# A two-layer encoder on one core: the exchange of the softmax's sums issued by ScalarE, the gate of heads 4 to 7 with its operands kept in SBUF, and another order of x's norms and of the second layer's transpositions

## The chip, the core and the metric

The kernel runs on one core of a Trainium2 chip. A core has a matrix engine (TensorE, PE in the profile), a vector engine (VectorE, DVE), a scalar engine (ScalarE, ACT), a general engine (GpSimd, POOL) and a synchronisation engine that here does little but issue transfers (SyncE, SP). Each engine works through its own instructions in order and stops at the first whose semaphore has not been reached; the instruction that issues a DMA is one of them. The tensors lie in SBUF (128 partitions); TensorE writes its results into banks of PSUM. The metric is the device time of one execution in microseconds, as the median of several runs.

## The reference

For 512 tokens of width 1024 two layers are computed, all in float32. Each normalises x, makes one wide projection, mixes heads, lets four heads attend to 256 memory tokens, gates everything and projects back. The first layer's mixer is the part that the change touches most: eight heads, each with three window attentions of different dilation, whose outputs are joined by a softmax over their log-sum-exps.

```python
o_g, l_g = dilated_window_attention(q[:, :, g], k[:, :, g], v[:, :, g], window, dilation)
...
o = jnp.stack(outs, axis=2)
w = jax.nn.softmax(jnp.stack(lses, axis=2), axis=2)
o = jnp.sum(w[..., None].astype(o.dtype) * o, axis=2)
...
y = jnp.concatenate([o_mix, o_mem], axis=-1) * jax.nn.silu(gate)
x = x + jnp.einsum('bse,ed->bsd', y, w_out[i])
```

The second layer's mixer is a grouped-query attention (8 query heads, 2 key heads) with rotary positions.

## The kernel before, in words

**Products.** A float32 product is made from three fast ones: each operand is split into a rounded part and a remainder ("hi" and "lo"). For a weight piece of 128x1024 (`wl`, loaded from DRAM) ScalarE makes the rounded part (`wh`, line 333, line 331 for the memory's weights) and VectorE the remainder (`wo`, line 347). TensorE then runs lines 178, 179 and 182: `wh` with the activations' two parts, `wo` with their rounded part. The rings of `wh` and `wo` hold four pieces each. Each chunk of 512 columns is computed with seven products in place of eight (the function `s_chunk`), whose summed weights GpSimd makes by accumulating DMAs (lines 260, 296, 306) and whose results ScalarE (line 415) and VectorE (lines 428, 438) take out of PSUM.

**Order.** Every engine's order is fixed when the program is written. The class `Driver` counts slots, about one weight piece each; work beside the projections sits in generators which give back how many slots are to pass until they go on (`yield 3`). In a slot `drv.soon` puts an operation at its beginning, `drv.late` at its end. The first layer goes through heads 0 to 7, then the gate of heads 4 to 7 (`b`), the gate of the memory's heads (`m`) and that of heads 0 to 3 (`a`); a head takes about 49 us.

**The exchange.** The three dilations of a head keep their tokens in two layouts across partitions: natural and strided by four. Each softmax needs the maxima and sums of both, so they are exchanged through a small DRAM buffer `ds`. VectorE packs them into `stp` (line 1494, 128 partitions x 16 numbers); SyncE writes both halves to `ds` (lines 1496 and 1497, 512 pieces of 8 bytes and 128 of 32 bytes), and `Y[3]` slots later reads them back in the other layout into `oth` (lines 1499 and 1500). The reads wait for the writes' landing. VectorE goes on from `oth` at line 1505. SyncE also issues nearly all loads of weights (line 260), the stores of the heads' outputs `od` (line 1353) and the loads of gathered values (lines 1483 to 1485), all in one order.

**The gate.** A head's output `o` goes to DRAM (`od`) and is loaded back when its gate is computed, unless it is in `DIRECT`: then it stays in SBUF. Line 911 multiplies two heads at once from a joint load, line 915 one head.

**Beginnings.** The first layer's activations are normalised in `setup` and `prep` (line 583 by VectorE), transposed, and combined for the seven products in `diffs_t` and `rest_t` (ScalarE lines 650, 655, 671, VectorE 675, 677, 672; tiles `f`, `fS` and their split parts `hS`). In the second layer `ev_rot` norms, rotates and transposes queries and keys (TensorE line 708, four 128x128 transpositions into one bank, then ScalarE line 1724 and VectorE line 1725).

Of the kernel before, what the change touches and what calls it, by code (L numbers as in the profile page):

```python
# [25 lines left out]
MEM_STEP = 1, 1  # L26
MEM_D = 4
PAUSE = 2
DIRECT, DIRECT_B = (6, 7), (3, 4, 5, 6, 7)
LO_K, TURN_K, HI_V, LO_V = (4, 4), (8, 5), (1, 6), (9, 2)  # L30
PD = 2
WARM = 6, 5
# [101 lines left out]
def trunk_kernel(ctx: ExitStack, tc: tile.TileContext, x, mem, wall, norm_g, mem_norm_g, gcol,  # L134
                 qn_a, kn_a, qn_b, kn_b, ident_d, mask_d, tab_a, tab_b, out):
    nc = tc.nc
# [515 lines left out]
    def diffs_t(H, low, c, view=same, turn=same, late=False):  # L652

        f22 = whole("22", c)
        A.copy(view(f22), turn(turn4(low[1], None, None)))
        p = turn(turn4(low[0], None, None))
        yield 1
        s1, s3 = whole("S1", c), whole("S3", c)
        V.tensor_tensor(view(s1), p, view(f22), ALU.subtract)
        V.tensor_tensor(view(s3), view(full["11", c]), p, ALU.subtract)  # L660
        hl = slot(H, "S1", c)
        if late:
            drv.late(lambda: split(*hl, s1))
        else:
            split(*hl, s1)
# [202 lines left out]
    def gates(od, o_done, o_here, direct, fused=False, turn=None):  # L868
# [3 lines left out]
        def gate(H, first, g, half=False):  # L872


            pre = {}
            if g < 2:
                yf[g] = [m4(name="yf") for _ in range(2)]
                if fused:
                    assert all(first + n in o_done for n in range(4))
                    for j in range(2):  # L880
                        pre[j] = m4(name="og").rearrange("p (h t) -> p h t", h=2)
                        nc.scalar.dma_start(pre[j], od[first + 2 * j:first + 2 * j + 2].rearrange("h p t -> p h t"))

            def ev(q, u, t):
                i, j = int(q[0]) - 1, int(q[1]) - 1
                h0, ts = first + 2 * j, slice(i * 256, (i + 1) * 256)
                hs, got, asked = (h0, h0 + 1), {}, []
                tv = t.rearrange("p (h t) -> p h t", h=2)

                def load():  # L890
                    if "o" not in got and all(h in o_done for h in hs):
                        asked.append(h0)
                        o = got["o"] = s2(name="og")
                        nc.sync.dma_start(o.rearrange("p (h t) -> p h t", h=2), od[h0:h0 + 2, :, ts].rearrange("h p t -> p h t"))
                        got[h0] = got[h0 + 1] = o.rearrange("p (h t) -> p h t", h=2)
                    for n, h in enumerate(hs):
                        if h in got:
                            continue
                        if h in o_here:
                            got[h] = o_here[h][:, None, ts].to_broadcast([128, 2, 256])  # L900
                        elif h in o_done and (hs[1 - n] in direct):
                            o = s2(name="og")[:, 0:256]
                            nc.sync.dma_start(o, od[h, :, ts])
                            asked.append(h)
                            got[h] = o[:, None, :].to_broadcast([128, 2, 256])

                def times(dst):
                    if "pre" in got:
                        V.tensor_tensor(dst.rearrange("p (h t) -> p h t", h=2), tv, got["pre"], ALU.mult)
                    elif "o" in got:  # L910
                        V.tensor_tensor(dst, t, got["o"], ALU.mult)
                    else:
                        dv = dst.rearrange("p (h t) -> p h t", h=2)
                        for n, h in enumerate(hs):
                            V.tensor_tensor(dv[:, n], tv[:, n], got[h][:, n], ALU.mult)

                if pre:
                    for h in hs:
                        got[h] = got["pre"] = pre[j][:, :, ts]
                else:  # L920
                    load()
                th = s2(name="th")
                A.activation(th, t, AF.Tanh, scale=0.5)
                yield 1
                V.scalar_tensor_tensor(t, th, 1.0, t, ALU.add, ALU.mult)
                yield 1
                if not all(h in got for h in hs):
                    load()
                    while not all(h in got for h in hs):
                        yield 1  # L930
                        asked.clear()
                        load()
                    if asked if fused else not all(h in o_here for h in hs):
                        yield 1
                if g < 2:
                    times(yf[g][j][:, i * 512:(i + 1) * 512])
                    y_done.add((g, i, j))
                    return
                times(t)
                if not fused:  # L940
                    yield 1
                ys[2 * j + i] = t

            s_chunk(256, H, ev, tokens=False, half=half, soon=g == 2, turn=turn)
# [265 lines left out]
    def prep():  # L1210

        for c in range(5):
            if c > 1:
                norm_2(xb[c - 1], n[c - 1], rows["x"])
            if 1 < c < 4:
                n[c] = norm_1(xb[c], c == 2)
            if 1 < c < 4:
                first_t(H, xb[c - 2], c - 2, by_class, from_rows)
            yield 1

        def forms(c):
            yield from diffs_t(H, xb[2 + c], c, by_class, from_rows)
            yield 3
            yield from rest_t(H, c, (2, 2, 2))

        drv.spawn(forms(1), 1)
        yield from forms(0)
# [32 lines left out]
    def square(b, j, act=True):  # L1260

        if act:
            A.activation(s2(name="sq"), mb[b][j], AF.Square, scale=1.0 / 32.0, accum_out=ss[b][:, j:j + 1])
        else:
            V.tensor_tensor_reduce(s2(name="sq"), mb[b][j], mb[b][j], 1.0 / 1024.0, 0.0, ALU.mult, ALU.add, ss[b][:, j:j + 1])
# [9 lines left out]
    def place_m(b, j, act=True):  # L1275

        p = turn4(mb[b][j], None, None)
        split(*[M.block(n, j, slice(b * 128, (b + 1) * 128)) for n in range(2)], p, act)
# [19 lines left out]
    def ahead(u, b):  # L1298

        if (u, b) == (0, 0):  # L1300
            square(1, 0)
            square(0, 1, False)
            place_m(1, 0)
            W.hi(True)
            W.hi(True)
        if (u, b) == (0, 1):
            place_m(0, 1)
            factor(0)
            square(1, 1, False)
            place_m(1, 1)  # L1310
            factor(1)
            n[0] = norm_1(xb[0])
            n[1] = norm_1(xb[1])
        if (u, b) == (1, 0):
            norm_2(xb[0], n[0], rows["x"])

    drv.spawn(prep(), PD)
    drv.spawn(setup(), SET_AT)
# [111 lines left out]
    def attn_a(h, qk0, qs, ks, v12, n_done):  # L1430
# [62 lines left out]
        oth = small.tile([128, 2, 4, 2], F32, tag="oth", name="oth", bufs=2)  # L1493
        V.tensor_copy(stp, st.rearrange("p o s b -> p o b s"))
        yield 1
        nc.sync.dma_start(nat_v[0], stp[:, 0])
        nc.sync.dma_start(str_v[1], stp[:, 1].rearrange("p b s -> p (b s)"))
        yield Y[3]
        nc.sync.dma_start(oth[:, 0], nat_v[1])
        nc.sync.dma_start(oth[:, 1].rearrange("p b s -> p (b s)"), str_v[0])  # L1500
        yield Y[4]
        own = stp.rearrange("p o b s -> p (o b) s")
        oth_ = oth.rearrange("p o b s -> p (o b) s")
# [210 lines left out]
        V.tensor_tensor(x[:, :, 64:128], ta[:, :, 64:128], sb[:, :, 0:64], ALU.add)  # L1714
        yield d[2]

    def ev_rot(t, qk, tab, hi, lo, d):
        n = t.shape[-1] // 128
        r = head_sq(t, n)
        yield d[0]  # L1720
        head_mul(t, r, n, dst=t)
        yield from rope_b(t, qk, tab, d)
        p = turn_h(t) if tab[1] > 1 else transpose4(t.rearrange("p (a e) -> p a e", e=128), n)[:, 0:n]
        drv.late(lambda: A.copy(hi, p))
        drv.soon(lambda: V.tensor_tensor(lo, p, hi.bitcast(F32), ALU.subtract))
        yield 1

    kbT = [m4(F32R, "kbT").rearrange("p (h t) -> p h t", h=2) for _ in range(2)]
    vb = [m4(F32R, "vb").rearrange("p (b e) -> p b e", b=4) for _ in range(2)]
    qs_b = [[[m4(F32R, "qb").rearrange("p (h t) -> p h t", h=4) for _ in range(2)] for _ in range(2)]]  # L1730
    k_done, q_done = {}, set()

    def ev_qkv(q, u, t):
        i, j = int(q[0]) - 1, int(q[1]) - 1
        b = 2 * i + u
        cs = slice(b * 128, (b + 1) * 128)
        if j:
            hi, lo = [v[:, b] for v in vb]
            A.activation(hi, t[:, 256:512], AF.Copy, scale=0.5)
            yield from ev_rot(t[:, 0:256], 1, (b, 1), *[v[:, :, cs] for v in kbT], YB["k"])  # L1740
            V.scalar_tensor_tensor(lo, t[:, 256:512], 0.5, hi.bitcast(F32), ALU.mult, ALU.subtract)
            k_done[b] = drv.slot
        else:
            cs = slice(u * 128, (u + 1) * 128)
            yield from ev_rot(t, 0, (b, 1), *[v[i][:, :, cs] for v in qs_b[0]], YB[0])
            q_done.update((0, b, j) for j in range(2))
# [204 lines left out]
```

## Time and profile before

| | |
|---|---|
| median of 3 runs | 934.84 us (933.46 to 935.6) |
| the profiled execution | 934.63 us |
| its span | 932.9 us, granted TensorE clock 0.999 |
| VectorE busy | 800.9 us, 86% of the span |
| ScalarE busy | 696.4 us, 75% |
| GpSimd busy | 361.2 us, 39% |
| share of the 16 DMA engines: SyncE's queue (q1), GpSimd's (q0), ScalarE's (q10) | 42.1%, 38.9%, 1.0% |

The span runs from the first to the last instruction of the profile; the profiled execution's own time is 1.7 us longer. Rows of the trace name start, duration, engine, line, operation and tiles (written one first); "ACTq" or "SPq" is an instruction that issues a transfer. In brackets stands the idle time ahead of an instruction and what ended it.

### The profile page before, as it was taken

What the parts mean: (1) busy time and instruction counts of PE and PEld (TensorE: products, weight loads), DVE (VectorE), ACT (ScalarE), POOL (GpSimd) and SP (SyncE); (2) the same over time, 40 slices, a digit from 0 to 9 for tenths busy, and PEclk for the clock granted to TensorE, in tenths of its full rate; (3) what the DMA queues carried; (4) which work ended last, traced back from release to release, by engine and by line L of the source; (5) the groups of instructions that cost most, each with busy time, mean ns of one, the idle gap of its engine ahead of it and who ended that gap; (6) DMA issues with size and microseconds to landing.
All of it is one profiled execution on the core that took longest, in us unless ns stands there. A gap on an engine that the chain in (4) does not pass through costs nothing.

```text
span 932.9 us, 16288 instructions
## 1 busy us (share of the span) xinstructions
PE 925.0 (99%) x5471; PEld 814.6 (87%) x5471; DVE 800.9 (86%) x1452; ACT 696.4 (75%) x1730; POOL 361.2 (39%) x504
## 2 busy tenths in 40 slices
PE   9999999999999999999999999999999999999998
PEld 7789888888888888888889998888988999999886
DVE  6999677878888888979798989999898998789977
ACT  7875789676868686867776667757879887789774
POOL 4311424556564646464746102234262440110122
PEclk9999999999999999999999999999999999999999
DMA  9999957968686878686867999999985686785777
GB/s 347 393 261 332 294 133 202 328 151 241 163 248 158 261 159 271 158 270 130 252 156 190 285 267 262 293 322 335 295 204 113 178 241 169 198 219 127 196 167 181
DMA packets 83723, 213.38 MB, mean 229 GB/s; under 512 B 18992, under 2 KB 26296, under 8 KB 83640
## 3 DMA queue, kind: packets, MB, share of 16 engines
q1 hardware_dynamic: 61288, 141.68, 42.1%
q0 software_dynamic: 20384, 67.12, 38.9%
q10 hardware_dynamic: 1968, 3.54, 1.0%
q8 instruction: 43, 0.70, 0.3%
q14 instruction: 40, 0.33, 0.1%
HBM read 163.23 MB, written 12.91 MB: 189 GB/s over the span
## 4 chain that ended last, share of the span: by engine, by line
PE 91%; DVE 4%; ACT 2%; issue 1%; DMA 1%; POOL 1%; SPq 0%; DVEq 0%; ACTq 0%; POOLq 0%
PE pj L178 24%; PE pj L179 24%; PE pj L182 24%; PE qT L708 3%; PE sa L1462 2%; PE oo L1571 2%; PE ptb L1780 1%; PE sa L1458 1%; DVE wo L347 1%; PE pt L1550 1%; PE ob L182 1%; PE ob L179 1%; PE ob L178 1%; PE sb L173 1%; PE sb L172 1%
## 5 line engine op out<-in xcount | busy, mean ns | idle before, releaser
L347 DVE TENSOR_TENSOR wo<-wl,wh 128x1024 fp32r<-128x1024 f32 x253 | 308.9, 1225 | 5.6 <-ACT wh L333 5.5
L333 ACT CAST wh<-wl 128x1024 fp32r<-128x1024 f32 x253 | 267.1, 1061 | 28.9 <-PE pj L179 19.6
L178 PE MATMUL pj<-wh,hS 128*128 128x512 f32 (+1 forms) x416 | 154.3, 380 | 0.4 <-DVE sn L438 0.4
L179 PE MATMUL pj<-wh,hS 128*128 128x512 f32 (+1 forms) x416 | 148.7, 366 | 0.0
L178 PE MATMUL pj<-wh,h 128*128 128x512 f32 (+1 forms) x312 | 115.3, 378 | 0.0
L179 PE MATMUL pj<-wh,h 128*128 128x512 f32 (+1 forms) x312 | 111.6, 366 | 0.0
L536 POOL TENSOR_TENSOR rstd<-mse,half 128x4 f32<-128x4 f32 (+2 forms) x98 | 102.4, 1045 | 8.2
L182 PE MATMUL pj<-wo,hS 128*128 128x512 f32 (+1 forms) x416 | 99.4, 365 | 0.0
L178 PEld LDWEIGHTS pj<-wh,hS 128*128 128x128 f32 x416 | 78.5, 189 | 11.8 <-issue 0.6
L179 PEld LDWEIGHTS pj<-wh,hS 128*128 128x128 f32 x416 | 78.7, 189 | 11.1
L535 POOL TENSOR_SCALAR mse<-hss 128x4 f32<-128x4 f32 (+1 forms) x88 | 46.8, 531 | 104.6 <-ACT junk L696 97.1
L182 PEld LDWEIGHTS pj<-wo,hS 128*128 128x128 f32 x416 | 72.5, 189 | 12.8
L696 ACT ACTIVATE junk<-sn 128x128 f32<-128x128 f32 x264 | 79.3, 311 | 3.2 <-DVE sn L428 3.2
L260 POOL DMA_DIRECT2D wl<-in_wall_dram x44 | 41.2, 965 | 97.0 <-DMA wl<-in_wall_dram 28.3
L1403 POOL TENSOR_TENSOR ta<-sn,tabs 128x128 f32<-128x128 f32 (+1 forms) x64 | 38.0, 600 | 104.3 <-DVE sn L701 80.4
L415 ACT COPY sn<-pj 128x512 f32<-128x512 f32 x122 | 67.2, 590 | 12.3 <-PE pj L182 12.3
L182 PE MATMUL pj<-wo,h 128*128 128x512 f32 (+1 forms) x312 | 74.5, 365 | 0.0
L306 POOL DMA_DIRECT2D wl<-wl x35 | 31.0, 896 | 106.3 <-DVE wo L347 44.2
L178 PEld LDWEIGHTS pj<-wh,h 128*128 128x128 f32 x312 | 59.0, 189 | 8.4 <-DVE sn L438 0.3
L179 PEld LDWEIGHTS pj<-wh,h 128*128 128x128 f32 x312 | 59.0, 189 | 8.3
L438 DVE TENSOR_TENSOR sn<-pj,sn 128x512 f32<-128x512 f32 x89 | 60.8, 684 | 6.0 <-PE pj L182 5.7
L296 POOL DMA_DIRECT2D wl<-wl x35 | 32.9, 974 | 78.3 <-DVE wo L347 25.8
(297 smaller groups left out, 2402.9 us busy)
## 6 DMA issues: line engine op xcount, KB each, us to landing
wl<-in_wall_dram SPq DMA_DIRECT2D x226, 512.0 KB, 8.2
wl<-wl POOLq DMA_DIRECT2D x70, 512.0 KB, 6.0
wl<-in_wall_dram POOLq DMA_DIRECT2D x48, 512.0 KB, 8.4
od<-o SPq DMA_DIRECT2D x10, 256.0 KB, 5.6
x<-in_x_dram SPq DMA_DIRECT2D x4, 512.0 KB, 8.2
v0r<-sn SPq DMA_DIRECT2D x8, 256.0 KB, 10.7
v0d<-v0r SPq DMA_DIRECT2D x4, 512.0 KB
og<-od ACTq DMA_DIRECT2D x4, 512.0 KB, 11.0
```

The costliest lines, as they stand in the source:

```text
L178: T.matmul(o, a, b, start=start, stop=False, skip_group_check=True)
L179: T.matmul(o, c, d, start=False, stop=False, skip_group_check=True)
L182: T.matmul(o, a, b, start=False, stop=stop, skip_group_check=True)
L260: queue.dma_start(t, wall[d], **how)
L333: A.copy(wh, self.tile[key])
L347: V.tensor_tensor(wo, self.tile[key], wh.bitcast(F32), ALU.subtract)
L415: A.copy(t_, b_)
L438: V.tensor_tensor(t_, b_, t_, ALU.subtract if q == "12" and late is None else ALU.add)
L535: G.tensor_scalar(e, ss, EPS, None, ALU.add)
L536: G.tensor_tensor(r, e, half[:, 0:n], ALU.pow)
L696: A.activation(jk, p[:, j * 128:(j + 1) * 128], AF.Square, scale=by, accum_out=ss[:, j:j + 1])
L1403: G.tensor_tensor(ta[:, 0:n], xn[:, 0:n, 0:32], ropeA[:, 0, b, s0:s0 + n], ALU.mult)
```

## The change

It has five parts.

1. The four DMAs of the exchange are issued by ScalarE (`nc.scalar`) in place of SyncE, at the same places in the slots, for all eight heads.
2. Head 5 joins `DIRECT`, so of heads 4 to 7 only head 4 goes through DRAM, and it is loaded once at the gate's start in place of two loads of a head pair's halves.
3. In the first microseconds: the second memory tile's placing (line 169) comes ahead of a square (line 1265), and x's second norm is applied together with the first (four times line 583 in a row).
4. `forms` combines the activations of the second half of x a slot later (`late`, `3 + c`, `2 - c`).
5. The second layer's transpositions move to the end of their slot (`drv.late`), and the last two key pairs share one bank and one ScalarE and one VectorE operation.

```diff
-DIRECT, DIRECT_B = (6, 7), (3, 4, 5, 6, 7)
+DIRECT, DIRECT_B = (5, 6, 7), (3, 4, 5, 6, 7)
...
-            pre = {}
+            pre, near = {}, dict(o_here)
+            if fused and g == 2:
+                for h in range(first, first + 4):
+                    if h in o_done:
+                        near[h] = s2(name="og")
+                        nc.sync.dma_start(near[h], od[h])
...
-            if c > 1:
+            if c > 2:
                 norm_2(xb[c - 1], n[c - 1], rows["x"])
...
-            yield from diffs_t(H, xb[2 + c], c, by_class, from_rows)
-            yield 3
-            yield from rest_t(H, c, (2, 2, 2))
+            yield from diffs_t(H, xb[2 + c], c, by_class, from_rows, late=True)
+            yield 3 + c
+            yield from rest_t(H, c, (2 - c, 2, 2))
...
             square(1, 0)
+            place_m(1, 0)
             square(0, 1, False)
-            place_m(1, 0)
...
         if (u, b) == (1, 0):
             norm_2(xb[0], n[0], rows["x"])
+            norm_2(xb[1], n[1], rows["x"])
...
-        nc.sync.dma_start(nat_v[0], stp[:, 0])
-        nc.sync.dma_start(str_v[1], stp[:, 1].rearrange("p b s -> p (b s)"))
+        nc.scalar.dma_start(nat_v[0], stp[:, 0])
+        nc.scalar.dma_start(str_v[1], stp[:, 1].rearrange("p b s -> p (b s)"))
         yield Y[3]
-        nc.sync.dma_start(oth[:, 0], nat_v[1])
-        nc.sync.dma_start(oth[:, 1].rearrange("p b s -> p (b s)"), str_v[0])
+        nc.scalar.dma_start(oth[:, 0], nat_v[1])
+        nc.scalar.dma_start(oth[:, 1].rearrange("p b s -> p (b s)"), str_v[0])
...
+        elif not qk:
+            drv.late(turned)
...
+        elif not pair:
+            pair += [drv.slot, at("qT").rearrange("p (u h t) -> p u h t", u=2, h=2), ta]
+        else:
+            assert pair[0] == drv.slot
+            for u, x in enumerate((pair[2], ta)):
+                for h in range(2):
+                    T.transpose(pair[1][:, u, h], x[:, h], ident)
```

Three places of ScalarE's order follow; "waits" names the semaphores of an instruction, DMAHW those of transfers issued by SyncE or ScalarE. First the slots of head 4 around the exchange, before (heads 0 to 5 all read so; `ks` is a scaled copy of a key transposition):

```order
L696 ACTIVATE junk,hss<-sn 128x128 [waits DVE_49,Activation_49]
L696 ACTIVATE junk,hss<-sn 128x128 [waits Activation_49] x3
L333 CAST wh<-wl 128x1024 [waits DMASW5_49,PE_49]
L333 CAST wh<-wl 128x1024 [waits DMASW6_49,DVE_49,PE_49]
L1414 ACTIVATE ks<-qT,gk 128x128 [waits PE_49]
L333 CAST wh<-wl 128x1024 [waits DMAHW1_49,DVE_49]
```

The same place in the changed kernel, whose line numbers are 6 higher here:

```order
L696 ACTIVATE junk,hss<-sn 128x128 [waits DVE_49,Activation_49]
L696 ACTIVATE junk,hss<-sn 128x128 [waits Activation_49] x3
L1502 DMA ds<-stp 128x4x2 [waits DMAHW1_49,DVE_49]
L1503 DMA ds<-stp 4x32x8 [waits DMAHW2_49]
L333 CAST wh<-wl 128x1024 [waits DMASW5_49,PE_49]
L333 CAST wh<-wl 128x1024 [waits DMASW6_49,PE_49]
L1505 DMA oth<-ds 128x4x2 [waits DMAHW3_49,DMAHW2_49]
L1506 DMA oth<-ds 128x1x8 [waits DMAHW4_49,DMAHW1_49]
L1420 ACTIVATE ks<-qT,gk 128x128 [waits PE_49]
L333 CAST wh<-wl 128x1024 [waits DVE_49]
```

The writes stand two weight casts ahead of the reads, and the reads wait for DMAHW1 and DMAHW2, which the writes set; the scaled key copy and all later casts stand behind them.

Second, ScalarE at head 7 in the changed kernel, where it also loads back the outputs of heads 0 to 3 (`og`), casts for the output projection (`y`, `yl`, `ylS`) and computes the gate's `th`:

```order
L887 DMA og<-od 128x2x512 [waits DVE_49] x2
L333 CAST wh<-wl 128x1024 [waits DMASW7_49]
L1502 DMA ds<-stp 128x4x2 [waits DMAHW5_49,DVE_49]
L1503 DMA ds<-stp 4x32x8 [waits DMAHW6_49]
L1037 CAST yl_6853<-sn 128x512 [waits DVE_49,Activation_49]
L1587 COPY o<-oo 128x512 [waits PE_49]
L415 COPY sn<-pj 128x512
L333 CAST wh<-wl 128x1024 [waits DMAHW0_49]
L928 ACTIVATE th<-sn 128x512 [waits DVE_49]
...
L1505 DMA oth<-ds 128x4x2 [waits DMAHW6_49,DMAHW0_49]
L1506 DMA oth<-ds 128x1x8 [waits DMAHW5_49,DMAHW1_49]
L1037 CAST ylS_6913<-yl 128x512 [waits DMASW1_49,DVE_49,Activation_49]
```

Before, the same rows stood there without the four exchange DMAs; now the writes follow two loads of 512 KB on ScalarE's own queue.

Third, ScalarE at the split of the first layer's combined activations (`hS_623` is the operand of the next products, of which `f_456` is the second half of x), before:

```order
L671 CAST hS_623<-f_390 128x4x128 [waits DVE_49]
L333 CAST wh<-wl 128x1024 [waits DMASW0_49,PE_49]
L671 CAST hS_623<-f_456 128x4x128 [waits DVE_49]
L333 CAST wh<-wl 128x1024 [waits DMASW1_49,PE_49]
L671 CAST hS_670<-f_388 128x4x128
```

and in the changed kernel:

```order
L671 CAST hS_623<-f_390 128x4x128 [waits DVE_49]
L333 CAST wh<-wl 128x1024 [waits DMASW0_49,PE_49]
L333 CAST wh<-wl 128x1024 [waits DMASW1_49,PE_49]
L671 CAST hS_666<-f_388 128x4x128 [waits DVE_49]
L671 CAST hS_623<-f_456 128x4x128 [waits DVE_49]
```

The cast of the second half (`hS_623<-f_456`) now stands behind one weight cast and behind the first half of the operand after it.

More of the change, by code (lines that the diff above doesn't have):

```diff
@@ L898, in load @@
                             continue
-                        if h in o_here:
-                            got[h] = o_here[h][:, None, ts].to_broadcast([128, 2, 256])
+                        if h in near or h in o_here:
+                            got[h] = (near if h in near else o_here)[h][:, None, ts].to_broadcast([128, 2, 256])
                         elif h in o_done and (hs[1 - n] in direct):
@@ L1310, in ahead @@
             place_m(1, 1)
-            factor(1)
             n[0] = norm_1(xb[0])
             n[1] = norm_1(xb[1])
+            factor(1)
         if (u, b) == (1, 0):
             norm_2(xb[0], n[0], rows["x"])
+            norm_2(xb[1], n[1], rows["x"])
     drv.spawn(prep(), PD)
@@ L1715, in rope_b, with ev_rot @@
         yield d[2]
-    def ev_rot(t, qk, tab, hi, lo, d):
+    def ev_rot(t, qk, tab, hi, lo, d, pair=None):
         n = t.shape[-1] // 128
@@ L1722, in ev_rot, with out, turned @@
         yield from rope_b(t, qk, tab, d)
-        p = turn_h(t) if tab[1] > 1 else transpose4(t.rearrange("p (a e) -> p a e", e=128), n)[:, 0:n]
-        drv.late(lambda: A.copy(hi, p))
-        drv.soon(lambda: V.tensor_tensor(lo, p, hi.bitcast(F32), ALU.subtract))
+        ta = t.rearrange("p (a e) -> p a e", e=128)
+        def out(p, hi=hi, lo=lo):
+            A.copy(hi, p)
+            drv.soon(lambda: V.tensor_tensor(lo, p, hi.bitcast(F32), ALU.subtract))
+        def turned():
+            out(transpose4(ta, n)[:, 0:n])
+        if tab[1] > 1:
+            p = turn_h(t)
+            drv.late(lambda: out(p))
+        elif not qk:
+            drv.late(turned)
+        elif pair is None:
+            p = transpose4(ta, n)[:, 0:n]
+            drv.late(lambda: out(p))
+        elif not pair:
[5 more added lines that the diff above has]
+                    T.transpose(pair[1][:, u, h], x[:, h], ident)
+            hl = [v.rearrange("p h (u t) -> p h u t", u=2) for v in both]
+            drv.late(lambda: out(pair[1].rearrange("p u h t -> p h u t"), *hl))
         yield 1
@@ L1731, in trunk_kernel @@
     k_done, q_done = {}, set()
+    last_k, both = [], [v[:, :, 256:512] for v in kbT]
     def ev_qkv(q, u, t):
@@ L1739, in ev_qkv @@
             A.activation(hi, t[:, 256:512], AF.Copy, scale=0.5)
-            yield from ev_rot(t[:, 0:256], 1, (b, 1), *[v[:, :, cs] for v in kbT], YB["k"])
+            yield from ev_rot(t[:, 0:256], 1, (b, 1), *[v[:, :, cs] for v in kbT], YB["k"], last_k if i else None)
             V.scalar_tensor_tensor(lo, t[:, 256:512], 0.5, hi.bitcast(F32), ALU.mult, ALU.subtract)
```

## The prediction

> **What bounds the kernel now.** I read the page's shares first, then the waits of TensorE alone.
>
> ```profile
> PE 925.0 (99%) x5471; PEld 814.6 (87%) x5471; DVE 800.9 (86%) x1452; ACT 696.4 (75%) x1730; POOL 361.2 (39%) x504
> ```
>
> TensorE is busy 925.0 of 932.9 us. The change takes no matmul away, so it can only win what TensorE waits, and any new wait of TensorE adds to the time in full. All its waits, by line and what ended them (us in total, times, longest):
>
> ```profile
> PE idle L1285 <- POOL tabs L550: 1.0, 1, 1.0
> PE pmt L839 <- DVE pmT L845: 0.8, 1, 0.8
> PE xT L589 <- ACT h L166: 0.6, 1, 0.6
> PE pj L179 <- DVE act L169: 0.6, 1, 0.6
> PE pj L178 <- DVE sn L438: 0.4, 1, 0.4
> PE pj L178 <- ACT wh L331: 0.4, 1, 0.4
> PE xT L589 <- issue: 0.2, 1, 0.2
> PE qT L708 <- DVE sn L1714: 0.2, 1, 0.2
> ```
>
> They sum to 4.2 us, all at the start or in the second layer; no head's exchange is among them. Whatever the change frees on SyncE, TensorE was not waiting for it. So the question is small gains against what the exchange may hold up on its new engine.
>
> **The change part by part.** The sum is made against the profiled execution's 934.63 us (span 932.9 and 1.7 around it), which is 0.2 us under the median of the runs shown.
>
> *The exchange, heads 0 to 5.* On SyncE at head 4 (start, duration):
>
> ```profile
> 395.42 0.38 SPq L1496 DMA_DIRECT2D ds<-stp  x1
> ...
> 396.53 0.40 SPq L260 DMA_DIRECT2D wl<-in_wall_dram  x1
> 399.32 0.33 SPq L1353 DMA_DIRECT2D od<-o  x1
> ...
> 400.21 0.45 SPq L1499 DMA_DIRECT2D oth<-ds  x1
> ```
>
> From write to read 4.8 us passed, and the read's semaphore is the write's landing. That blocked only an engine that issues transfers. On ScalarE the same wait blocks casts. Its rows at that place, with VectorE's and TensorE's that hang on them:
>
> ```profile
> 399.75 0.31 ACT L696 ACTIVATE junk<-sn 128x128 f32<-128x128 f32 x1
> ...
> 400.37 1.06 ACT L333 CAST wh<-wl 128x1024 fp32r<-128x1024 f32 x1 [0.22 <-PE pj L179]
> 403.09 1.06 ACT L333 CAST wh<-wl 128x1024 fp32r<-128x1024 f32 x1 [1.66 <-PE pj L179]
> 406.94 0.37 ACT L1414 ACTIVATE ks<-qT,gk 128x128 f32<-128x128 f32 x1 [2.80 <-PE qT L708]
> ```
>
> ```profile
> 407.35 0.35 DVE L1415 TENSOR_SCALAR ks<-qT,gk 128x128 f32<-128x128 f32 x1 [1.07 <-ACT ks L1414]
> 407.61 0.68 DVE L438 TENSOR_TENSOR sn<-pj,sn 128x512 f32<-128x512 f32 x1
> ```
>
> ```profile
> 410.63 0.40 PE L178 MATMUL pj<-wh,hS 128*128 128x512 f32 x1
> ```
>
> In the new order the writes follow the last L696, so they are issued at about 400.2 and 400.6, where they were ready at 395.4; the reads follow the second weight cast (ends 404.15), and L1414 the reads. L1414 feeds VectorE's L1415, behind which L438 (ends 408.29) empties the bank that the matmul at 410.63 writes. So L1414 may come 410.63 - 408.29 = 2.34 us later than 406.94, at 409.28. The two issues ahead of it take 0.45 and, by the same instruction on SyncE, about 0.56: the write must have landed by about 408.2, **7.6 us after its issue**. Whatever it is later, TensorE waits, six times, since heads 0 to 5 have the same order.
>
> How long does it take? The lower bound is SyncE's 4.8 us: nothing waits. But SyncE itself was stopped then and the DMA engines ran empty, which its first two rows show: 1 load in 4 us. At 400 to 411 they are full, and the 4.8 us no longer fit. The queues in 401 to 411 us (packets, MB, share of the 16 engines), then what loads issued on SyncE at 401 to 405 took to land, then ScalarE's own loads of `og` over the whole run:
>
> ```profile
> q0 software_dynamic: 287, 1.05, 54.5%
> q1 hardware_dynamic: 1208, 1.74, 50.9%
> ...
> wl<-in_wall_dram SPq DMA_DIRECT2D x3, 512.0 KB, 11.2
> ```
>
> ```profile
> og<-od ACTq DMA_DIRECT2D x4, 512.0 KB, 11.0
> ```
>
> The write is small in bytes but not in packets: in 396 to 397.5 us the two writes are nearly all of what q1 moved, and in 543 to 544 us all three queues are busy:
>
> ```profile
> q1 hardware_dynamic: 670, 0.02, 24.5%
> ```
>
> ```profile
> q0 software_dynamic: 23, 0.09, 47.8%
> q1 hardware_dynamic: 27, 0.11, 29.9%
> q10 hardware_dynamic: 28, 0.06, 17.1%
> ```
>
> The second block shows the three queues served in equal numbers of packets, whatever their size: 28 of ScalarE's (q10) to 27 and 23. At that rate, 28 / 16 = 1.75 packets per engine and us, the 670 / 16 = 42 packets per engine would take 24 us. That is the upper end by price alone; but q0 and q1 have only so much to move, and after some 10 us they are through, so 411 us for the last packet and 2.8 for its landing (on SyncE its packets lay in that window of 396 to 397.5, and its reads went out at 400.2) is the latest that I count: 413.8, a stall of 413.8 - 408.2 = 5.6 us. Between 0 and 5.6 I take the nearest rows, the 11.2 us of what was issued at that very place and the 11.0 of ScalarE's own queue: landed at 400.6 + 11.2 = 411.8, **3.6 us of TensorE's wait per head, 21.6 us for six**.
>
> The Trainium skill (DMA: Bandwidth & Descriptors, "Queues, rings and completion order") says that each DMA engine takes turns between the queues packet by packet, a packet there holding some 9 to 17 descriptors. By that alone a write of 42 small descriptors per engine would be through in three to five turns, and the estimate would come nearer to the lower end; the equal counts above agree with the turns, and nothing in this trace shows how many descriptors one turn takes. This is the second rival.
>
> *Head 6* has two more pairs of ScalarE's operations between writes and reads, so I cost it at 0 (up to 3).
>
> *Head 7.* ScalarE's rows, and TensorE's next group:
>
> ```profile
> 538.22 1.56 ACTq L882 DMA_DIRECT2D og<-od  x1
> ...
> 544.79 1.14 ACT L957 CAST y<-yf 128x512 fp32r<-128x512 f32 x2
> 547.41 0.62 ACT L1032 CAST ylS<-yl 128x512 fp32r<-128x512 f32 x1 [1.49 <-issue]
> ...
> 549.54 0.59 ACT L415 COPY sn<-pj 128x512 f32<-128x512 f32 x1
> ```
>
> ```profile
> 552.22 0.28 PE L178 MATMUL pj<-hS,wh 128*128 128x256 f32 x1
> ```
>
> The writes stand behind two loads of 512 KB on the same queue, which land 11 us after 538.22, at 549.2; the writes' packets and landing, 2.8 us by the row above, give 552.0. ScalarE is through with `y` at 545.9 and blocked until then; it issues the reads (1.0), and from `ylS` to the end of L415 it needs 550.13 - 547.41 = 2.72, so L415 ends at 555.7. That eviction frees the bank of the matmul at 552.22: **3.5 us** (0 if the writes overtake the loads, 6 if weights share their way).
>
> *What else waits for the exchange.* `oth` comes later, but VectorE uses it at 414.42 at head 4, and that is shifted with TensorE: 0, up to 2 each.
>
> ```profile
> 414.42 0.15 DVE L1505 TENSOR_TENSOR nmM<-stp,oth 128x8 f32<-128x8 f32 x1
> ```
>
>  SyncE's loads are issued earlier: 0, since no wait for a load is in the list. Head 5's store and three loads of the gate go: 0 likewise, and one 128x512 multiplication becomes two of 128x256 on VectorE at two places.
>
> *The first 35 us.* The earlier L169 and the second norm shorten the waits of 0.6 and 0.2 us at most. But both lie ahead of the 0.6 us at xT L589 <- ACT h L166, where VectorE's norm of the next x tile ends late for a reason that does not move (loads land, then a square, then the norm). What is won ahead is waited there: 0 (at most -0.6).
>
> *The split of the activations.* ScalarE and TensorE around 54 us:
>
> ```profile
> 51.70 0.62 ACT L671 CAST hS<-f 128x512 fp32r<-128x512 f32 x1 [1.49 <-DVE f L675]
> 52.99 1.05 ACT L333 CAST wh<-wl 128x1024 fp32r<-128x1024 f32 x1 [0.66 <-PE pj L182]
> 53.94 0.62 ACT L671 CAST hS<-f 128x512 fp32r<-128x512 f32 x1
> ```
>
> ```profile
> 53.80 0.47 PE L178 MATMUL pj<-wh,hS 128*128 128x512 f32 x1 [0.38 <-DVE sn L438]
> ...
> 55.01 0.39 PE L179 MATMUL pj<-wh,hS 128*128 128x512 f32 x1
> ```
>
> The two L438 now run ahead of VectorE's second sum, so the wait of 0.38 goes. But the cast of 51.70, operand of the later matmuls of this group, now stands behind the one of 52.99 and another L671: 52.99, 53.94, then about 54.46 to 55.08, and VectorE's remainder ends 0.7-0.9 later, about 55.95. The matmul at 55.01 needs it: **+0.9 us** (between -0.4 and +1.5).
>
> *The second layer.* The transpositions that move go behind matmuls that are ready, so the 0.2 at qT L708 <- DVE sn L1714 goes; one VectorE and one ScalarE operation fewer. The 0.8 at pmt L839 lies ahead of the merged pair and stays: **-0.2**.
>
> Sum: 934.6 + 21.6 + 3.5 + 0.9 - 0.2 = **960.4 us**.
>
> **The rivals.**
>
> *The small writes pass quickly* in heads 0 to 5 (within 7.6 us). For it: 11.2 and 11.0 us are landings of large loads, and the write alone took 4.8. Against it: the equal turns. Then only head 7 and the split remain: 934.6 + 3.5 + 0.9 - 0.2 = 938.8, and with half of head 7's price 937.0.
>
> *Faster: ScalarE's wait is covered everywhere.* The place is L1414 at each head and `ylS` at head 7; it decides at 7.6 us per write, and at head 7 at a landing before 548.5. For it: ScalarE has 1.66 and 2.80 us of idle time in these rows, and is busy only 75%. Then the waits of 0.6, 0.2, 0.4 and 0.2 can go, and if the split's cast comes in time as well, 934.6 - 1.4 = 933.2; with the 0.8 of L839 and the 0.6 of xT besides, 931.8. Most of this is faster by over 0.2%.
>
> *Nothing changes*: the gains and head 7 cancel, 933 to 936.5.
>
> The skill's first page (Trainium Kernel Development and Optimization, "Key Constraints") says that transfers issued by SyncE, ScalarE and GpSimd run on the same 16 engines and interleave, and that another issuing engine saves only the time of issuing. By it the change could win no transfer time; the equal counts agree.
>
> **How the numbers follow.** A measurement of this kernel can tell 0.2%, 1.9 us, from no change. Forecast (ScalarE held at each head, 1 to 7 us): 0.62, from 942 to 978; quick writes: 0.17, from 935.5 to 941, of which a quarter is within 0.2%; faster: 0.14; no change: 0.07, of which all counts as same. Slower 0.62 + 0.13 = 0.75, same 0.04 + 0.07 = 0.11, faster 0.14. The range leaves out the faster case and little more: 935 to 978.
>
> **What would show it.** In the changed kernel's waits: TensorE waiting for VectorE's L438 and ScalarE near each head's exchange, some 3 to 4 us, six times, and ScalarE's idle time ahead of its exchange reads ended by `ds`. Right in part: such waits at head 7 alone. Wrong: no TensorE wait there, the write landing within 7.6 us, or a gain in places that I cost at 0.

## The result, and the profile after

The changed kernel takes **981.89 us** (median of 4 runs, 980.88 to 983.58) against 935.21 us of before in the same session: a ratio of 1.0506, 95% interval 1.0493 to 1.052. It is 46.7 us slower where 25.8 were forecast (960.4 against the 934.6 that the sum starts from), and 3.9 us above the range's upper end. The profiled execution has a span of 981.8 us, 48.9 more than before, and a mean granted clock of 0.980.

First the page of the changed kernel: busy times, the granted TensorE clock in 40 slices (tenths) and the chain that ended last.

```profile
PE 939.7 (96%) x5471; PEld 824.6 (84%) x5471; DVE 800.7 (82%) x1453; ACT 695.5 (71%) x1729; POOL 358.9 (37%) x504
...
PEclk9999999999999798998999999999999999999999
...
PE 76%; DMA 13%; DVE 5%; ACT 4%; issue 2%; ACTq 1%; POOL 0%; SPq 0%; DVEq 0%; POOLq 0%
PE pj L178 20%; PE pj L182 20%; PE pj L179 20%; DMA ds<-stp 7%; DMA wl<-in_wall_dram 3%; PE qT L708 2%; PE sa L1468 1%; PE ptb L1811 1%; PE oo L1577 1%; PE sa L1464 1%; DVE wo L347 1%; ACT wh L333 1%; DMA v<-v0d 1%; PE pt L1556 1%; ACT junk L696 1%
```

The 4 KB writes `ds<-stp`, which did not show in the chain before, hold 7% of it. And TensorE runs the same 5471 matmuls, but is busy 14.7 us longer; the row of clocks shows dips in three slices between 319 and 466 us.

TensorE's waits in the changed kernel (us in total, times, longest):

```profile
PE pj L178 <- DVE sn L438: 31.0, 5, 8.1
PE pj L178 <- ACT sn L415: 3.4, 1, 3.4
PE pj L178 <- ACT hS L671: 1.1, 1, 1.1
PE idle L1290 <- POOL tabs L550: 1.0, 1, 1.0
PE xT L589 <- ACT h L166: 0.8, 1, 0.8
PE pj L179 <- DVE hS L672: 0.3, 1, 0.3
PE pj L179 <- DVE act L169: 0.2, 1, 0.2
```

They sum to 37.8 us against 4.2. The rise of 33.6 and the 14.7 of longer busy time make 48.3 of the span's 48.9 us. So there are two parts: waits, as forecast, and slower matmuls, which were not.

The longest wait, at head 2. ScalarE's rows of the changed kernel around its exchange:

```profile
309.40 0.38 ACTq L1502 DMA_DIRECT2D ds<-stp  x1
...
309.82 0.85 ACTq L1503 DMA_DIRECT2D ds<-stp  x1
310.77 1.06 ACT L333 CAST wh<-wl 128x1024 fp32r<-128x1024 f32 x1 [0.87 <-PE pj L179]
312.83 1.06 ACT L333 CAST wh<-wl 128x1024 fp32r<-128x1024 f32 x1 [1.01 <-PE pj L179]
326.15 0.39 ACTq L1505 DMA_DIRECT2D oth<-ds  x1
326.63 0.55 ACTq L1506 DMA_DIRECT2D oth<-ds  x1
327.22 0.37 ACT L1420 ACTIVATE ks<-qT,gk 128x128 f32<-128x128 f32 x1 [13.33 <-DMA v<-v0d]
```

ScalarE does nothing from 313.9 to 326.1: the read at L1505 waits. The row puts the wait down to `v<-v0d`, which landed about then; what L1505 waits for by its semaphore is the write of L1503, issued at 309.8, whose last piece arrives 16.3 us later, at 326.1. TensorE meanwhile:

```profile
320.15 0.39 PE L179 MATMUL pj<-wh,hS 128*128 128x512 f32 x1
328.63 0.80 PE L178 MATMUL pj<-wh,hS 128*128 128x512 f32 x1 [8.09 <-DVE sn L438]
329.22 0.63 PE L179 MATMUL pj<-wh,hS 128*128 128x512 f32 x1
...
334.74 0.40 PE L178 MATMUL pj<-wh,hS 128*128 128x512 f32 x1
```

Behind the wait the same matmul takes 0.63 us, until 334.7, when it is back at 0.40. The windows of all engines (the last three columns are the granted clock, the share of the DMA engines, GB/s) show why:

```profile
320.00:324.00 4.00, 0.54 (x3) 0.10 (x1) 0.00 (x0) 0.00 (x0) 0.00 (x0) 1.00 1.03 315
324.00:328.00 4.00, 0.00 (x0) 0.00 (x0) 0.38 (x2) 0.78 (x2) 0.00 (x0) 0.56 0.35 91
328.00:332.00 4.00, 3.37 (x8) 2.71 (x9) 4.00 (x9) 4.00 (x15) 1.95 (x2) 0.50 0.66 230
332.00:336.00 4.00, 4.00 (x13) 3.15 (x13) 2.71 (x9) 1.97 (x9) 3.75 (x6) 0.66 0.86 294
336.00:340.00 4.00, 4.00 (x24) 3.32 (x23) 3.06 (x5) 2.71 (x7) 1.09 (x2) 1.00 0.00 1
```

Some 4 us into the wait TensorE's clock falls to 0.50, and it is back at 1.00 only some 6 us after work has begun again. Behind the six waits of this kernel TensorE worked 27.7 us at 0.50, which costs half of that, 13.8 of the 14.7 us. The Trainium skill (TensorE: Matmul & The Clock Gate, "Part 1: The HAM clock gate (the "warmup" mystery)") says that the clock is halved after about 3.4 us without work and restored after as much work. This trace agrees in kind, with 4 and 6 us; but below the clock also fell behind some waits of 1.8 us, which that sentence does not give, and there the measurement decides.

### The profile page after: what moved, and what is told of

Same layout as the page of the kernel before. It is cut to its first block, busy times and chain, and to the rows that moved or that the text cites. A ratio compares the mean times of both kernels' runs of the same rounds, so it can differ in the third digit from the quotient of the medians.

```text
span 981.8 us, 16276 instructions
## 1 busy us (share of the span) xinstructions
PE 939.7 (96%) x5471; PEld 824.6 (84%) x5471; DVE 800.7 (82%) x1453; ACT 695.5 (71%) x1729; POOL 358.9 (37%) x504
## 4 chain that ended last, share of the span: by engine, by line
PE 76%; DMA 13%; DVE 5%; ACT 4%; issue 2%; ACTq 1%; POOL 0%; SPq 0%; DVEq 0%; POOLq 0%
PE pj L178 20%; PE pj L182 20%; PE pj L179 20%; DMA ds<-stp 7%; DMA wl<-in_wall_dram 3%; PE qT L708 2%; PE sa L1468 1%; PE ptb L1811 1%; PE oo L1577 1%; PE sa L1464 1%; DVE wo L347 1%; ACT wh L333 1%; DMA v<-v0d 1%; PE pt L1556 1%; ACT junk L696 1%
## 5 line engine op out<-in xcount | busy, mean ns | idle before, releaser
L178 PE MATMUL pj<-wh,hS 128*128 128x512 f32 (+1 forms) x416 | 159.9, 393 | 32.1 <-DVE sn L438 31.0
L179 PE MATMUL pj<-wh,hS 128*128 128x512 f32 (+1 forms) x416 | 153.0, 376 | 0.3 <-DVE hS L672 0.3
L178 PEld LDWEIGHTS pj<-wh,hS 128*128 128x128 f32 x416 | 81.5, 196 | 46.5 <-DVE sn L438 33.2
L182 PE MATMUL pj<-wo,hS 128*128 128x512 f32 (+1 forms) x416 | 103.5, 377 | 0.0
L536 POOL TENSOR_TENSOR rstd<-mse,half 128x4 f32<-128x4 f32 (+2 forms) x98 | 100.4, 1025 | 8.2
L179 PEld LDWEIGHTS pj<-wh,hS 128*128 128x128 f32 x416 | 81.4, 196 | 12.4 <-DVE hS L672 0.6
L182 PEld LDWEIGHTS pj<-wo,hS 128*128 128x128 f32 x416 | 75.3, 196 | 14.0
L415 ACT COPY sn<-pj 128x512 f32<-128x512 f32 x122 | 67.2, 589 | 11.7 <-PE pj L182 11.5
L306 POOL DMA_DIRECT2D wl<-wl x35 | 31.0, 896 | 108.0 <-DVE wo L347 49.5
L1420 ACT ACTIVATE ks<-qT,gk 128x128 f32<-128x128 f32 x32 | 10.8, 363 | 81.8 <-DMA v<-v0d 46.8
L438 DVE TENSOR_TENSOR sn<-pj,sn 128x512 f32<-128x512 f32 x89 | 60.6, 682 | 7.0 <-PE pj L182 6.7
## 6 DMA issues: line engine op xcount, KB each, us to landing
og<-od ACTq DMA_DIRECT2D x4, 512.0 KB, 13.4
```

Of the source, the lines that this page charges most:

```text
L178: T.matmul(o, a, b, start=start, stop=False, skip_group_check=True)
L179: T.matmul(o, c, d, start=False, stop=False, skip_group_check=True)
L182: T.matmul(o, a, b, start=False, stop=stop, skip_group_check=True)
L415: A.copy(t_, b_)
L438: V.tensor_tensor(t_, b_, t_, ALU.subtract if q == "12" and late is None else ALU.add)
L536: G.tensor_tensor(r, e, half[:, 0:n], ALU.pow)
```

## The experiments

The kernel before ran beside each; its medians lay between 934.26 and 934.54 us.

**The exchange on SyncE, all else as changed.**

```diff
-        nc.scalar.dma_start(nat_v[0], stp[:, 0])
+        nc.sync.dma_start(nat_v[0], stp[:, 0])
```

(and so the other three)

> The changed kernel with only the four exchange DMAs issued by SyncE again; everything else as changed. Theory A (all of the loss is TensorE's waits at the exchange on ScalarE, 31.0 us at heads 1 to 5 and 3.4 at head 7, and the half-clock stretches behind them, 14.7 us of longer TensorE work): the other parts cost +1.0 at the split of the activations and win some 1.8 in the other waits, so 933 to 935 us, TensorE busy 925, clock 0.999. Rival B (another part of the change, the gate or the forms, holds part of the loss): over 938.

934.7 us, ratio 0.9993 (0.9982 to 1.0004). TensorE's waits:

```profile
PE idle L1290 <- POOL tabs L550: 1.0, 1, 1.0
PE xT L589 <- ACT h L166: 0.9, 1, 0.9
PE pj L178 <- ACT hS L671: 0.8, 1, 0.8
PE pj L179 <- DVE hS L672: 0.4, 1, 0.4
PE pj L179 <- DVE act L169: 0.2, 1, 0.2
```

The whole loss goes with the engine that issues the exchange. The four other parts together cannot be told from no change.

**Only the exchange on ScalarE, all else as before.** The same four lines the other way round in the kernel before.

> The kernel before with only the exchange moved to ScalarE. Theory A: the whole loss, 980 to 984 us, five waits of TensorE of 5 to 8 us ended by L438, granted clock 0.98. Rival B (the loss needs the other parts as well): under 970.

986.7 us, ratio 1.0551 (1.0515 to 1.0588), a little above Theory A's range, at clock 0.978, with waits of 31.5 us at L438 (five of 5.3 to 9.1 and the old 0.4 at the split) and 6.0 at head 7's L415. The exchange alone makes the loss. Whether it makes more of it than with the other parts is not shown: the intervals of the two ratios overlap.

**Writes on SyncE, reads on ScalarE.**

> The changed kernel with the writes issued by SyncE again and the reads left on ScalarE. Theory A (what holds ScalarE is the landing of writes that are issued 5 us later there and go packet by packet in turns with the full queues): the writes are issued when ready and land some 5 us later, before ScalarE comes to the reads; ScalarE waits for nothing, 933 to 938 us. Rival C (issuing and waiting on ScalarE costs by itself, wherever the write comes from): over 950.

941.78 us, ratio 1.0067 (1.0042 to 1.0092), above Theory A's range and far from Rival C. No wait at L438 is left: at heads 0 to 6 the writes have landed before ScalarE comes to the reads. At head 7 ScalarE still waits 5.8 us for them, and TensorE 2.0 us at L415. The reads, now late on ScalarE, land when VectorE wants them; TensorE waits 1.5 us behind VectorE at the scores (L1464). The rows below show who waited for `oth` in this run (line, us, times):

```profile
  DVE nmM L1511: 10.5, 6
  ACT e L1516: 2.5, 2
```

**Writes on ScalarE, reads on SyncE.**

> The changed kernel with the writes on ScalarE and the reads issued by SyncE again. Theory A (ScalarE loses its time in the wait ahead of the reads): the writes land as late, 10 to 16 us after issue, but the one that waits is SyncE; no wait of TensorE at L438, 934 to 942 us, some of it from oth coming late (VectorE's L1511 at 414 in a head whose read would start at 413 to 416). Rival D (late data of the exchange, not ScalarE's stop, is what TensorE pays): over 960.

936.19 us, ratio 1.0011 (0.9999 to 1.0023). ScalarE issues the same writes at the same place and loses nothing: its head 2,

```profile
302.65 0.89 ACTq L1503 DMA_DIRECT2D ds<-stp  x1
303.63 1.05 ACT L333 CAST wh<-wl 128x1024 fp32r<-128x1024 f32 x1 [0.91 <-PE pj L179]
305.66 1.06 ACT L333 CAST wh<-wl 128x1024 fp32r<-128x1024 f32 x1 [0.97 <-PE pj L179]
309.52 0.37 ACT L1420 ACTIVATE ks<-qT,gk 128x128 f32<-128x128 f32 x1 [2.80 <-PE qT L708]
```

and SyncE's, which waits in its place:

```profile
302.31 1.52 SPq L260 DMA_DIRECT2D wl<-in_wall_dram  x1
315.30 0.38 SPq L1505 DMA_DIRECT2D oth<-ds  x1
```

What TensorE pays in the changed kernel is thus the stop of the engine that casts, not the issues. It is not late data either: VectorE waits for `oth` 3.3 us in the changed kernel and 3.5 us in this run. That data can cost it when they come later still, the run with later reads below shows.

A second thing stands in these rows: from write to read 12.6 us passed here, 16.3 in the changed kernel. In this run SyncE issued one load and then stood still until 315; in the changed kernel it went on, with four weight loads and two of gathered values:

```profile
309.48 4.19 SPq L260 DMA_DIRECT2D wl<-in_wall_dram  x4
318.36 0.38 SPq L1489 DMA_DIRECT2D v<-v0d  x1
318.79 0.82 SPq L1490 DMA_DIRECT2D v<-v0d  x1
```

At each of heads 1 to 5 the second write landed 3.7 to 6.4 us later in the changed kernel than in this run.

**The second write on more engines.** It has an outer size of 4; here it goes as four DMAs of 32 rows.

```diff
-        nc.scalar.dma_start(str_v[1], stp[:, 1].rearrange("p b s -> p (b s)"))
+        for i in range(4):
+            nc.scalar.dma_start(str_v[1][i], stp[32 * i:32 * i + 32, 1].rearrange("p b s -> p (b s)"))
```

> The changed kernel with the second write (128 pieces of 32 bytes, in one DMA of 4 outer rows) issued as four DMAs of 32 rows each. Theory F (that write's outer size of 4 puts its pieces on few DMA engines, where they queue behind the first write's and last longest: it lands last at every head): its landing falls from 13.4-16.3 us to that of the first write, 9 to 13, and each of the five waits gets some 1 to 5 us shorter, less 1.5 us of added issues: 955 to 978 us. Rival G (the queues as a whole are full until then, on every engine): unchanged or slower by the issues, 980 to 992.

966.48 us, ratio 1.0345 (1.033 to 1.0361). The waits at L438 are halved, against 31.0:

```profile
PE pj L178 <- DVE sn L438: 15.7, 6, 4.3
```

So about half of the waiting goes with the shape of one small write, which here lands with the first one. In the changed kernel it landed 7.6 and 6.5 us behind the first write at heads 2 and 3, and 0.2 to 1.2 us behind it at heads 1, 4 and 5. The queues of the changed kernel in 318 to 324 us, at the end of that tail at head 2, show how it crawls:

```profile
q1 hardware_dynamic: 351, 1.16, 56.0%
q0 software_dynamic: 137, 0.50, 43.5%
q10 hardware_dynamic: 15, 0.00, 0.2%
```

15 packets in 6 us, where 610 of ScalarE's 660 had started in 309 to 315 us. The Trainium skill's way of counting engines (DMA: Bandwidth & Descriptors, "Why a DMA increments its semaphore by 16 and not by 1") has the outer dimension set how many engines a transfer uses; by it this write would use 4 in place of 16, which is an estimate. The trace agrees: beside one right after the issue, the write's semaphore gets 4 arrivals, that of the first write 16. At head 2 three of the 4 came 6.4 to 7.5 us after the issue, and the last after 16.3.

**The reads two slots later.**

```diff
-Y, Y_LAST = [3, 2, 2, 2, 3, 2, 2, 1, 1, 1], [2, 2, 1, 1, 2, 1, 1, 1, 1, 1]
+Y, Y_LAST = [3, 2, 2, 4, 1, 2, 2, 1, 1, 1], [2, 2, 1, 1, 2, 1, 1, 1, 1, 1]
```

> The changed kernel with the reads of heads 0 to 6 two slots later (the fourth entry of Y from 2 to 4, the fifth from 3 to 1, so that everything behind keeps its slot). Theory A (the loss is the landing minus the place of the reads, and a half clock only behind waits of several us): two slots are some 6 us, so the waits of 5.2 to 8.1 us fall to 0 to 2 and leave the clock at 1.00; oth then lands some 2 us after its read, near VectorE's use. 938 to 950 us, granted clock over 0.995. Rival E (the later reads stop ScalarE as long, only at another place, since a stopped ScalarE holds back the weights' casts wherever it stops): over 965.

973.42 us, ratio 1.0432 (1.0411 to 1.0453): Theory A's number missed, and the time lies where Rival E put it. The wait at L438 is gone, and another stands in its place, at the scores of the next attention:

```profile
PE sa L1464 <- DVE qk L1426: 19.6, 6, 5.5
```

But it is not ScalarE's stop at another place, as Rival E had it. VectorE now stands still until `oth` lands; the rows are all its waits for `oth` in this run, and head 2:

```profile
DVE nmM L1511 <- DMA oth<-ds: 34.3, 7, 7.8
```

```profile
329.67 0.17 DVE L1511 TENSOR_TENSOR nmM<-stp,oth 128x8 f32<-128x8 f32 x1 [7.83 <-DMA oth<-ds]
...
338.02 0.43 DVE L1426 TENSOR_SCALAR qk<-qT,gk 128x128 f32<-128x128 f32 x1
```

From 329.7 on VectorE works without a pause to L1426, for which TensorE waits 5.5 us. Reads that are late enough thus cost TensorE by their data, 19.6 us here, what earlier ones cost it by ScalarE's stop: the expectation had put `oth` near VectorE's use, and it came up to 7.8 us after it.

**A stop of ScalarE without transfers.** The exchange is on SyncE; at the reads' place of heads 0 to 5, ScalarE makes 22, 30 or 46 copies that nothing uses.

```diff
+        if h < 6:
+            jk = small.tile([128, 128], F32, tag="junk", name="junk", bufs=2)
+            for _ in range(30):
+                A.copy(jk, ident)
```

> The changed kernel with the exchange on SyncE and, where the reads stood, 30 small copies (128x128) on ScalarE at heads 0 to 5, whose results nothing uses: a stop of ScalarE of known length without any transfer. Each copy some 0.25 us, so 7.5 us; 2.8 of it fits ScalarE's idle time there and 2.3 the slack behind it, so TensorE waits some 2.4 us six times. Theory H (a half clock follows only a long wait): 934.7 + 14 = 949, clock over 0.995. Rival I (each wait, short or long, costs the clock, or the loss is a matter of the transfers): longer by over 5 us than the sum of its TensorE waits, or no loss at all.

974.86 us, 40.2 more than without copies. The copies took 0.33 us each, longer than assumed, so the waits were 4.4 us, not 2.4. Beyond their 26.5 us lie 13.7, which by its words is Rival I; but these were long waits, so the run does not part it from Theory H.

> As the run with 30 copies, with 46: some 4 us more stop per head, so waits of 6.4 us six times. Theory H: the waits (38 us) plus a half clock for 4 to 6 us behind each, 2 to 3 us per head: 934.7 + 38 + 15 = 988 us, clock 0.98 or less. Rival I (the clock's loss comes with the full DMA queues and not with the wait): 934.7 + 38 = 973 us at clock 1.00.

1008.74 us at clock 0.970. The waits were 9.7 us, not 6.4, so both numbers missed; but the clock fell, with the exchange on SyncE, and Rival I, which had it at 1.00, is out.

> As the run with 30 copies, with 22. From 30 (six waits of 4.43 us) and 46 (9.69) each copy is 0.33 us, so 22 give six waits of about 1.8 us, 10.8 in all. Theory H (the half clock follows only waits beyond some 2 us): 934.7 + 10.8 = 945.5 us, clock 1.00, TensorE busy 925. Rival I (the charge on the clock is the same for each wait, about 2.2 us, as after 4.43): 959 us.

952.82 us, between the two forecasts. TensorE's busy time by the page, and its waits at L438, for 22, 30 and 46 copies in turn:

```profile
PE 931.2 (98%) x5471; PEld 816.4 (86%) x5471; DVE 799.9 (84%) x1453; ACT 734.1 (77%) x1861; POOL 368.9 (39%) x504
```

```profile
PE pj L178 <- DVE sn L438: 10.8, 6, 1.8
```

```profile
PE 938.2 (96%) x5471; PEld 822.2 (85%) x5471; DVE 799.5 (82%) x1453; ACT 748.8 (77%) x1909; POOL 359.9 (37%) x504
```

```profile
PE pj L178 <- DVE sn L438: 26.5, 6, 4.4
```

```profile
PE 941.3 (93%) x5471; PEld 824.3 (82%) x5471; DVE 799.9 (79%) x1453; ACT 777.3 (77%) x2005; POOL 360.2 (36%) x504
```

```profile
PE pj L178 <- DVE sn L438: 58.1, 6, 9.7
```

With the exchange on SyncE and no copies TensorE was busy 925.2 us. So with six waits of 1.8, 4.4 and 9.7 us its matmuls took 6.0, 13.0 and 16.1 us longer. For the two longer waits that is 2.2 and 2.7 us per wait: a charge per wait rather than a share of it, and it comes without any slow transfer. Neither Theory H nor Rival I holds for the shortest wait: after the first of the six, at 217 us, the clock fell, after the second it did not. The two windows behind them:

```profile
218.00:222.00 4.00, 4.00 (x13) 3.17 (x12) 3.65 (x11) 4.00 (x15) 3.40 (x5) 0.59 1.07 338
...
271.00:275.00 4.00, 4.00 (x21) 3.34 (x20) 3.65 (x8) 4.00 (x14) 3.79 (x5) 1.00 1.07 367
```

In that run the clock fell behind two of the six waits, for 3.41 us each, which is 3.4 of its 6.0 us; where the other 2.6 come from is not shown.

What decides between two waits of 1.8 us stays open, but the trace's record of the clock gives a hint. In all these runs the stretches at 0.50 behind waits are 3.41, 6.83 or 10.24 us long, whole multiples of 3.41, and in each run their beginnings lie a whole number of such steps apart (in the changed kernel at 266.44 and 324.47 us, 17 steps). Of the six waits of 1.8 us the two that brought the clock down lay whole inside one step of this grid; three of the others lay across a border of two steps, but one, at 424 to 426 us, lay inside a step as well.

**The exchange on SyncE and the split in its old order.** What is left of the change is the start, the gate and the second layer.

```diff
-            yield from diffs_t(H, xb[2 + c], c, by_class, from_rows, late=True)
-            yield 3 + c
-            yield from rest_t(H, c, (2 - c, 2, 2))
+            yield from diffs_t(H, xb[2 + c], c, by_class, from_rows)
+            yield 3
+            yield from rest_t(H, c, (2, 2, 2))
```

> The changed kernel with the exchange on SyncE and the split of the activations in its old order (diffs and rests as before). What is left of the change is the start, the gate and the second layer's transpositions. Theory J (the new order at the split costs 0.8 us net, the shared bank and the start win 1.7): 932.5 to 934 us, TensorE's waits at hS L671 and L672 (1.2 us) gone, that at L438 (0.4) back, some 0.1 to 0.2% under the kernel before. Rival K (none of these matter): within 0.1%, no difference from the run with the exchange on SyncE.

933.96 us, ratio 0.999 (0.9977 to 1.0002). The waits at L671 and L672 are gone as expected, and the median is the lowest of all; but the interval reaches over 1, so that it beats the kernel before is not shown.

## Why the prediction was right, and where it failed

*The mechanism of the wait held.* TensorE waits for L438 behind a ScalarE that waits for the write's landing. That was the forecast's case, and runs with the exchange, its writes and its reads moved one by one show it; the rival of a covered wait is out. The time was not right: the measured parts are 31.0 + 3.4 + 1.0 - 1.0 - 0.8 = 33.6 us of waits and 14.7 of slower matmuls, against 25.8 in the sum.

*The step that failed first: "any new wait of TensorE adds to the time in full".* A wait costs more than its length. The matmuls behind it run at half clock for several us; in the changed kernel that is nearly all of the 14.7 us of longer matmul time, a term that the sum did not have and without which the time would have stayed in the range. The trace of before could hardly show it, since its longest wait was 1.0 us. It follows from the rule of the Trainium skill cited above (TensorE: Matmul & The Clock Gate, Part 1), and it was not weighed. The runs with copies show that the wait alone does it.

*The second: "3.6 us of TensorE's wait per head, 21.6 us for six".* Measured were 31.0 us at five heads, 5.2 to 8.1 each, and none at head 0. The step that failed is the landing of 11.2 us, and there are two reasons. The 11.2 us were the landing of loads, which come in 16 arrivals, where the write that lands last comes in 4: spreading it halved the waits, as its run shows. And the cap of 413.8 took the other queues to be through after 10 us; with SyncE free they were fed on, and that write landed 13.4 to 16.3 us after its issue at heads 1 to 5, against 7.2 to 12.6 in the run in which SyncE stood still. That lies between the 11.2 taken and the 24 that the price per packet of three busy queues gave.

*The rival of quick small writes* came about at head 0 alone: the writes landed within 4.9 us there, and the two other queues moved 0.51 MB in 205 to 211 us, against 1.04 in 309 to 315 at head 2. At head 2 most small packets did pass quickly, 610 in those 6 us to 206 and 144 of the other queues, so the equal turns of the sum's upper end (28 to 27 and 23) did not hold there. But the landing is that of the last packet.

*Head 7:* 3.5 us forecast, 3.4 measured, with some luck: the loads ahead landed 13.4 us after their issue, not 11, and the write 0.4 us behind them, not 2.8. *Head 6:* 0, and no wait there.

*The split:* +0.9 forecast. The waits at L671 and L672 (1.4 together) less the 0.4 at L438 make +1.0. The size was right, the place not quite: 1.1 of it is a matmul that waits for ScalarE's cast itself, and only 0.3 are VectorE's remainder, for which the forecast had it wait.

*The first 35 us:* 0 forecast. The waits for L169, L331 and the issue went from 1.2 to 0.2, the one at L589 rose from 0.6 to 0.8; together that is -0.8, so most of the gain ahead was kept. In the other runs with this start these waits sum to 0.4 to 1.9 us, against 1.8 before, so the size is not firm. The change also puts `factor(1)` behind the two first norms there, which its description leaves out.

*The second layer:* -0.2 forecast, -1.0 measured: the 0.8 at `pmt` went as well. Its place in TensorE's order stayed, but two transpositions now share a bank, and one bank fewer is waited for. In every run with this part that wait is gone, and in the run without it, with the exchange alone moved, it stands. The link to the bank is read from the order and was not tried.

## What to carry to other kernels

A DMA that waits for another's landing should stand on an engine with nothing behind it that the bottleneck needs: count the instructions queued behind the waiting one, and take the landing under load, with the outer size of the small transfer, not that of an idle moment. Putting the dependent DMA later is no cure by itself: its data then come late for the engine that uses them. Freeing one issuing engine also feeds its queue, and what it then issues can hold up the transfer that was moved. A new wait of TensorE of some 2.4 us or more is to be charged with its length and, here, 2 to 3 us for the half clock behind it.

## What the runs showed of the hardware that was not expected

TensorE's clock fell to 0.50 at each of the 31 waits of 2.4 us or more in these runs, and the charge hardly grew with the wait: 2.2 us for waits of 4.4 us, 2.7 for 9.7. Of the 13 waits of 1.5 to 2.2 us three were followed by a fall. The stretches at 0.50 last whole multiples of 3.41 us. And a write of 4 KB took 16.3 us from issue to landing between full queues where in the kernel before loads of 512 KB took 11.2.
